# One decoder layer on one core: operand tiles moved to start addresses that differ by multiples of 512 bytes, and parts of two small computations moved off VectorE

## The chip, the cores and the metric

The kernel runs on one core of a Trainium2 chip. The time is that of one execution on the device in microseconds (us); the median of several executions is compared. The engines are named as the profile names them: PE is TensorE's matmuls and PEld its weight loads, DVE is VectorE, ACT is ScalarE, POOL is GpSimd, SP is the queue that issues most DMAs.

## The reference

One decoder layer for 1024 tokens of width 1024, all in float32: two token mixers side by side (a convolution module and an attention with forget gates), a gated sum of both, cross-attention into 256 memory tokens, and a mixture of 16 experts. The two parts that the change rewrites are the layernorm in the convolution module and the logarithm of the forget gates:

```python
def conformer_conv(u_glu, dw_w, dw_b, ln_g, ln_b, pw_w):
    a, gate = jnp.split(u_glu, 2, axis=-1)
    u = a * jax.nn.sigmoid(gate)
    u = lax.conv_general_dilated(u, dw_w[:, None, :], ..., feature_group_count=CONV_DIM) + dw_b
    u = jax.nn.silu(layernorm(u, ln_g, ln_b))
    return u @ pw_w
...
logf = jax.nn.log_sigmoid(f_logit.astype(jnp.float32) + fox_bf[l].astype(jnp.float32))
...
c = jnp.cumsum(logf, axis=1).transpose(0, 2, 1)   # added to the scores of the attention
```

The convolution has 512 channels and 31 taps. The rest of the layer is what the names say: `proj = h @ w_in` gives the inputs of both mixers and their gates, then come `fox_attention`, `cross_attention` and `hierarchical_moe`.

## The kernel before

Activations lie transposed, channels on the 128 partitions and tokens along the row, so that a weight tile of 128x128 is the stationary operand of a matmul and 512 tokens stream past it. Each float32 matrix is split into a rounded part and a rest (`hi` and `lo`, type float32r), and each product is three matmuls (lines 137 to 139: hi by hi, hi by lo, lo by hi). `hh` and `hl` are the two parts of the normed input, 8 tiles each of 4096 bytes per partition; `w_hi` and `w_lo` are the two parts of one weight tile. A column tile of `w_in` is so 2 halves of tokens x 8 x 3 = 48 matmuls of 512 columns. The weight arrives by DMA in `w_raw`; ACT rounds it (line 129), and the rest is subtracted on POOL or DVE (lines 131, 133). `w_hi` and `w_lo` have two buffers each.

Stages in time: the input is read and normed; 19 column tiles of `w_in` (up to about 263 us) for the convolution's input and gate, the convolution's output gate (`gc`), and the first head pair's queries, keys and values; the pointwise product of the convolution (`conv_pw_w`, up to about 312 us); the attention of 8 heads, with the remaining 17 column tiles of `w_in` laid between (up to 666 us); the branch and output products, cross-attention, router and experts.

The convolution runs beside the 19 column tiles. Channels lie in four blocks c = 0 to 3. Blocks 0, 2 and 3 are summed tap by tap on DVE, in PSUM (line 373, `ps_cva<-u,dw_w,ps_cva`). Block 1 is summed in SBUF by a pair: ACT multiplies (line 368, `pj`) and POOL adds (line 369, `oc`). POOL's queue also holds the subtraction of each weight tile (line 131, `w_lo`) and, once, the DMA that stores the running sum of the forget gates (line 417, `c_dram<-ncum`). Each engine works its own queue in order; the order is fixed when the program is built, by a scheduler with priorities, and stands on each engine as shown in the section on the change. DVE also takes every projection's result out of PSUM (line 217, two PSUM buffers `ps_lin`), so a late line 217 holds PE back.

The forget gates (lines 403 to 416) use 8 partitions x 1024 elements: bias, absolute value, exponential, logarithm, correction, and a running sum on DVE. The layernorm (lines 440 to 474) sums the four blocks into `lsum` (442, 443, 448), lets PE sum over partitions (450), subtracts the mean (452), squares on ACT (454, 457), adds the squares up in `lsum` on DVE (458), sums them over partitions with matmuls of one column (462), works out the reciprocal root in small steps (464, 160 to 162, 143 to 145), spreads it over the partitions (468, 470), scales (472), applies silu (473) and splits the result into `yh` and `yl` (474 through 129, 131, 133), which the product with `conv_pw_w` reads.

Where tiles start in SBUF: pools are filled one after the other, each tile behind the last. The small tiles at the head of `hpool` (`g_mem`, `dw_w`, `dw_b`, `ln_g`, `ln_b`, `bf8`: 8, 124, 4, 4, 4 and 1 elements per partition) push all that follows to odd places. Start addresses in the built program, as the remainder by 512: `w_hi` and `w_lo` 256; `hh` and `hl` 416; `ah`, `al` (branch product), the inputs of the cross-attention's query and of half of its output product 480; `yh` 128; `mgh`, `mgl` (output product) 256. In the experts the moving weights `gu` and the stationary `xgT` are both at 480, the moving `dn` is at 256 (for the last expert at 480) and the stationary `uh`, `ul` at 480.

## Time and profile before

| | us |
|---|---|
| three runs | 1240.29, 1238.8, 1247.19 |
| median | 1240.29 |
| the profiled execution | 1246.51 |
| its span (first to last instruction) | 1244.7 |
| mean granted TensorE clock, share of full speed | 0.981 |

The profiled execution holds 1.8 us outside its span and is 6.2 us above the median. Durations below are its own. A matmul's listed time runs from its start to its modelled end and overlaps the next one, so the pace of a stream of matmuls is read from starts. In the windows, busy times of an engine are its instructions' union; a window that PE fills is not proof that PE runs at its best pace. The granted clock is a share of 2.4 GHz: 1.00 is that level, and half of it is the level of 1.2 GHz.

### The profile page before, as it was taken

What the parts mean: (1) busy time and instruction counts of PE and PEld (TensorE: products, weight loads), DVE (VectorE), ACT (ScalarE), POOL (GpSimd) and SP (SyncE); (2) the same over time, 40 slices, a digit from 0 to 9 for tenths busy, and PEclk for the clock granted to TensorE, in tenths of its full rate; (3) what the DMA queues carried; (4) which work ended last, traced back from release to release, by engine and by line L of the source; (5) the groups of instructions that cost most, each with busy time, mean ns of one, the idle gap of its engine ahead of it and who ended that gap; (6) DMA issues with size and microseconds to landing.
All of it is one profiled execution on the core that took longest, in us unless ns stands there. A gap on an engine that the chain in (4) does not pass through costs nothing. (4 is left out here: it accounts for less than half of the span.)

```text
span 1244.7 us, 17029 instructions
## 1 busy us (share of the span) xinstructions
PE 1174.6 (94%) x6125; PEld 908.6 (73%) x6126; DVE 857.4 (69%) x1584; ACT 626.8 (50%) x1057; POOL 397.7 (32%) x270
## 2 busy tenths in 40 slices
PE   7999999989999999999999999999997798999996
PEld 3677877768877777787888787787764576767773
DVE  5499999863978778791234854665887785776665
ACT  6334663531655555472332343552752575776765
POOL 3328994111010010101011575265015023333343
PEclk9999999989999999999999999999998899999999
DMA  5211134126211111111344453234266889999977
GB/s 205 73 38 43 58 102 152 52 84 217 82 58 41 46 55 48 37 47 53 102 135 149 141 162 109 77 111 130 68 201 219 264 241 306 311 311 293 314 181 282
DMA packets 57466, 174.10 MB, mean 140 GB/s; under 512 B 7992, under 2 KB 11080, under 8 KB 57376
## 3 DMA queue, kind: packets, MB, share of 16 engines
q1 hardware_dynamic: 49680, 149.76, 36.2%
q0 software_dynamic: 7696, 23.20, 8.0%
q8 instruction: 50, 0.82, 0.3%
q14 instruction: 40, 0.33, 0.1%
HBM read 136.92 MB, written 36.01 MB: 139 GB/s over the span
## 5 line engine op out<-in xcount | busy, mean ns | idle before, releaser
L131 POOL TENSOR_TENSOR w_lo<-w_raw,w_hi 128x1024 fp32r<-128x1024 f32 x58 | 140.6, 2425 | 471.8 <-ACT w_hi L129 462.0
L137 PE MATMUL ps_lin<-hh,w_hi 128*128 128x512 f32 x560 | 226.5, 404 | 1.0 <-DVE u L351 1.0
L139 PE MATMUL ps_lin<-hh,w_lo 128*128 128x512 f32 x560 | 225.1, 402 | 1.7 <-POOL w_lo L131 1.6
L138 PE MATMUL ps_lin<-hl,w_hi 128*128 128x512 f32 x560 | 226.1, 404 | 0.0
L129 ACT ACTIVATE w_hi<-w_raw 128x1024 fp32r<-128x1024 f32 (+1 forms) x100 | 92.1, 921 | 212.3 <-PE ps_lin L138 158.6
L139 PEld LDWEIGHTS ps_lin<-hh,w_lo 128*128 128x128 f32 x560 | 105.8, 189 | 28.2 <-POOL w_lo L131 3.9
L137 PEld LDWEIGHTS ps_lin<-hh,w_hi 128*128 128x128 f32 x560 | 106.1, 190 | 26.5 <-issue 2.7
L138 PEld LDWEIGHTS ps_lin<-hl,w_hi 128*128 128x128 f32 x560 | 106.0, 189 | 24.8 <-issue 1.8
L373 DVE SCALAR_TENSOR_TENSOR ps_cva<-u,dw_w,ps_cva 128x1024 f32<-128x1024 f32 x90 | 111.7, 1280 | 0.3
L369 POOL TENSOR_TENSOR oc<-oc,pj 128x512 f32<-128x512 f32 x60 | 80.8, 1398 | 14.4 <-ACT pj L368 14.4
L133 DVE SCALAR_TENSOR_TENSOR gu<-e_raw,gu 128x1024 fp32r<-128x1024 f32 x64 | 77.5, 1223 | 4.6 <-ACT gu L129 0.6
L129 ACT ACTIVATE gu<-e_raw 128x1024 fp32r<-128x1024 f32 x64 | 67.5, 1059 | 8.3 <-PE ps_lin L139 6.7
L137 PE MATMUL ps_lin<-gu,xgT 128*128 128x512 f32 x144 | 58.5, 406 | 4.1 <-ACT xgT L129 4.1
L368 ACT ACTIVATE pj<-u,dw_w 128x512 f32<-128x512 f32 x60 | 42.2, 719 | 36.8 <-POOL oc L369 36.7
L133 DVE SCALAR_TENSOR_TENSOR dn<-d_raw,dn 128x1024 fp32r<-128x1024 f32 x32 | 39.0, 1225 | 29.4 <-ACT dn L129 26.8
L557 ACT ACTIVATE sc<-sc,mns 128x128 f32<-128x128 f32 (+3 forms) x64 | 49.4, 773 | 15.7 <-DVE mns L553 15.3
L138 PE MATMUL ps_lin<-gu,xgT 128*128 128x512 f32 x144 | 57.1, 397 | 0.0
L139 PE MATMUL ps_lin<-gu,xgT 128*128 128x512 f32 x144 | 56.9, 395 | 0.0
L133 DVE SCALAR_TENSOR_TENSOR pl<-ps_tra,ph 128x512 fp32r<-128x512 f32 (+1 forms) x80 | 49.1, 636 | 9.8 <-ACT ph L129 8.7
L1294 POOL DMA_INDIRECT xg<-h_dram,ids x29 | 33.2, 1144 | 67.1 <-PE ps_sco L1070 24.3
L129 ACT ACTIVATE ph<-ps_tra 128x512 fp32r<-128x512 f32 (+1 forms) x80 | 41.8, 552 | 23.9 <-PE ps_tra L570 23.1
L570 PE MATMUL ps_tra<-ident,sc 128*128 128x128 f32 x288 | 47.9, 276 | 4.1 <-DVE sc L560 4.1
(475 smaller groups left out, 2860.5 us busy)
## 6 DMA issues: line engine op xcount, KB each, us to landing
e_raw<-in_w_gu SPq DMA_DIRECT2D x64, 512.0 KB
w_raw<-in_w_in SPq DMA_DIRECT2D x36, 512.0 KB
d_raw<-in_w_dn SPq DMA_DIRECT2D x32, 512.0 KB
w_raw<-in_w_out SPq DMA_DIRECT2D x16, 512.0 KB
xT<-in_xT SPq DMA_DIRECT2D x16, 256.0 KB
gc_dram<-gc SPq DMA_DIRECT2D x8, 512.0 KB
gc<-gc_dram SPq DMA_DIRECT2D x8, 512.0 KB
mc_dram<-gc SPq DMA_DIRECT2D x8, 512.0 KB
```

The source lines that it names most:

```text
L129: order["split"] = A.activation(hi, src, AF.Copy, scale=scale)
L131: G.tensor_tensor(lo, src, hi.bitcast(F32), op=OP.subtract)
L133: V.scalar_tensor_tensor(lo, src, scale, hi.bitcast(F32), op0=OP.mult, op1=OP.subtract)
L137: TE.matmul(ps, lh, rh, start=first, stop=False)
L138: TE.matmul(ps, lh, rl, start=False, stop=False)
L139: return TE.matmul(ps, ll, rh, start=False, stop=last)
L368: A.activation(pj, uj, AF.Copy, scale=dw_h[:, c, j:j + 1])
L369: G.tensor_tensor(co[c][:, ns], co[c][:, ns], pj, op=OP.add)
L373: V.scalar_tensor_tensor(sums, u[c][:, j:j + T], dw_h[:, c, j:j + 1], sums, op0=OP.mult, op1=OP.add)
L557: A.activation(sc[:, :nk], sc[:, :nk], AF.Exp, scale=-1.0, bias=mns[:, nch - 1:nch], accum_out=sm)
L570: TE.transpose(pt[:, s_], pr[i][:, blk(j)], ident)
L1294: G.indirect_dma_start(out=XG[e, h][:n], out_offset=None, in_=src, in_offset=bass.IndirectOffsetOnAxis(ap=idx, axis=0))
```

## The change

The small tiles move into one tile `edge` of 56 elements per partition at the right end of SBUF, and `dw_w` is padded to 512 bytes. `mns`, `sm`, `lss` and `xss` get widths or counts that keep later tiles at the same remainder. In the built program nearly all large tiles then start at remainder 256: `hh`, `hl`, `ah`, `al`, `yh`, the cross-attention's inputs, `xgT`, `gu`, `uh`, `ul`, `dn`; `yl` starts at 0, 128, 256 and 384, and `w_hi`, `w_lo`, `mgh`, `mgl` stay at 256. The forget gates' bias, relu and the addition of 1 become ACT's; the addition of the relu becomes the second operand of the running sum. The layernorm's first two sums go to POOL, block 3 is read from PSUM, the squares are no longer added on DVE but each is summed by PE into the same PSUM columns (8 groups of 4 matmuls of one column, before 2 groups), and all eight subtractions that make `yl` go to POOL.

```diff
+    edge = ctx.enter_context(tc.tile_pool(name="edge", bufs=1, side="right")).tile([P, 56], F32, name="edge")
+    g_mem, dw_b, ln_g, ln_b = edge[:, 0:8], edge[:, 8:12], edge[:, 12:16], edge[:, 16:20]
+    bf8, nbf8 = edge[:HEADS, 20:21], edge[:HEADS, 21:22]
...
+    dw_w = hpool.tile([P, 4 * 32], F32, name="dw_w")[:, :4 * TAPS].rearrange("p (c j) -> p c j", c=4)
...
-        V.tensor_scalar(z, z, bf8, None, op0=OP.add)
         e = cv.tile([HEADS, T], F32, name="e", tag="yl", bufs=4)
-        A.activation(e, z, AF.Abs)
+        A.activation(e, z, AF.Abs, bias=bf8)
+        A.activation(z, z, AF.Relu, scale=-1.0, bias=nbf8)
         A.activation(e, e, AF.Exp, scale=-1.0)
         w1 = cv.tile([HEADS, T], F32, name="w1", tag="yl", bufs=4)
-        V.tensor_scalar(w1, e, 1.0, None, op0=OP.add)
+        A.activation(w1, e, AF.Identity, bias=1.0)
         ln = cv.tile([HEADS, T], F32, name="ln", tag="yl", bufs=4)
         A.activation(ln, w1, AF.Ln)
         V.scalar_tensor_tensor(w1, w1, 1.0, e, op0=OP.subtract, op1=OP.subtract)
         V.tensor_tensor(ln, ln, w1, op=OP.subtract)
-        V.tensor_scalar(z, z, -1.0, 0.0, op0=OP.mult, op1=OP.max)
-        V.tensor_tensor(ln, ln, z, op=OP.add)
         ncum = cv.tile([HEADS, T], F32, name="ncum", tag="yl", bufs=4)
-        V.tensor_tensor_scan(ncum, ln, ln, 0.0, OP.add, OP.bypass)
+        V.tensor_tensor_scan(ncum, ln, z, 0.0, OP.add, OP.add)
         G.dma_start(c_dram, ncum)
...
-            V.tensor_tensor(s, co[0], co[2], op=OP.add)
-            V.tensor_tensor(s, s, co[3], op=OP.add)
+            G.tensor_tensor(s, co[0], co[2], op=OP.add)
+            G.tensor_tensor(s, s, co[1], op=OP.add)
...
-                V.tensor_tensor(s[:, ns], s[:, ns], co[1][:, ns], op=OP.add)
+                V.tensor_tensor(s[:, ns], acc[3][:, ns], s[:, ns], op=OP.add)
                 ps = bank("acc")
                 TE.matmul(ps, ones, s[:, ns], start=True, stop=True)
                 for c in range(4):
                     V.scalar_tensor_tensor(co[c][:, ns], ps, -1.0 / 512, co[c][:, ns], op0=OP.mult, op1=OP.add)
+                    sq = cv.tile([P, HALF], F32, name="lsq", tag="pj", bufs=2)
+                    A.activation(sq, co[c][:, ns], AF.Square)
...
-                        V.tensor_tensor(s[:, ns], s[:, ns], sq, op=OP.add)
...
+                        pair = bank("cva", [P, T])
+                        ps2 = pair[:, HALF:]
+                    for t in range(4):
+                        TE.matmul(ps2[:, t:t + 1], sq[:, blk(t)], ones[:, 0:1], start=c + t == 0, stop=c + t == 6)
...
-                    split(yh[c][:, ns], yl[c][:, ns], co[c][:, ns], lo_eng=G if c % 2 else V)
+                    split(yh[c][:, ns], yl[c][:, ns], co[c][:, ns], lo_eng=G)
...
-                    mns = fx.tile([P, 2], F32, name="mns", tag="mns", bufs=4)
+                    mns = fx.tile([P, 16], F32, name="mns", tag="mns", bufs=4)
...
-                    sm = fx.tile([P, 1], F32, name="sm", tag="sm", bufs=4)
+                    sm = fx.tile([P, 16], F32, name="sm", tag="sm", bufs=4)[:, :1]
```

The order of the queues changes in three places that the prediction speaks of. In the changed kernel lines from 76 on are numbered a little higher (131 is there 135, 369 is 373, 417 is 419, 137 to 139 are 141 to 143, 217 is 221).

First, POOL's queue where block 1's taps begin. Before, the DMA of the forget gates' sum stands behind twelve additions:

```order
L131 TENSOR_TENSOR w_lo<-w_raw,w_hi 128x1024 [waits DMAHW2_49,PE_49,Activation_49]
L369 TENSOR_TENSOR oc<-oc,pj 128x512 [waits Activation_49] x4
L131 TENSOR_TENSOR w_lo<-w_raw,w_hi 128x1024 [waits DMAHW3_49,PE_49,Activation_49]
L369 TENSOR_TENSOR oc<-oc,pj 128x512 [waits Activation_49] x8
L417 DMA c_dram<-ncum 8x1024 [waits DMASW0_49,DVE_49]
L131 TENSOR_TENSOR w_lo<-w_raw,w_hi 128x1024 [waits DMAHW4_49,PE_49,Activation_49]
```

Now the same place in the changed kernel:

```order
L135 TENSOR_TENSOR w_lo<-w_raw,w_hi 128x1024 [waits DMAHW2_49,PE_49,Activation_49]
L419 DMA c_dram<-ncum 8x1024 [waits DMASW0_49,DVE_49]
L373 TENSOR_TENSOR oc<-oc,pj 128x512 [waits Activation_49] x2
L135 TENSOR_TENSOR w_lo<-w_raw,w_hi 128x1024 [waits DMAHW3_49,PE_49,Activation_49]
L373 TENSOR_TENSOR oc<-oc,pj 128x512 [waits Activation_49] x10
L135 TENSOR_TENSOR w_lo<-w_raw,w_hi 128x1024 [waits DMAHW4_49,PE_49,Activation_49]
```

The DMA, which waits for DVE, moved ahead of the twelve additions.

Second, DVE's queue at the end of block 3's taps, with the projections' results (`gc`, `qt`) between. Before:

```order
L217 TENSOR_TENSOR gc<-ps_lin,r 128x512
L373 SCALAR_TENSOR_TENSOR ps_cva<-u,dw_w,ps_cva 128x1024
L442 TENSOR_TENSOR lsum<-oc 128x1024
L373 SCALAR_TENSOR_TENSOR ps_cva<-u,dw_w,ps_cva 128x1024 x2
L217 TENSOR_TENSOR gc<-ps_lin,r 128x512
L373 SCALAR_TENSOR_TENSOR ps_cva<-u,dw_w,ps_cva 128x1024 x4
L217 TENSOR_TENSOR gc<-ps_lin,r 128x512
L373 SCALAR_TENSOR_TENSOR ps_cva<-u,dw_w,ps_cva 128x1024
L443 TENSOR_TENSOR lsum<-lsum,oc 128x1024
L448 TENSOR_TENSOR lsum<-lsum,oc 128x512 x2
L217 TENSOR_TENSOR qt<-ps_lin,r 128x512
```

In the changed kernel, from the same half of `gc` (the 14th of 16) on:

```order
L221 TENSOR_TENSOR gc<-ps_lin,r 128x512
L377 SCALAR_TENSOR_TENSOR ps_cva<-u,dw_w,ps_cva 128x1024 x4
L221 TENSOR_TENSOR gc<-ps_lin,r 128x512
L377 SCALAR_TENSOR_TENSOR ps_cva<-u,dw_w,ps_cva 128x1024 x2
L450 TENSOR_TENSOR lsum<-ps_cva,lsum 128x512 x2
L221 TENSOR_TENSOR gc<-ps_lin,r 128x512
L454 SCALAR_TENSOR_TENSOR oc<-ps_acc,oc 128x512 x5
```

Six taps instead of eight stand behind that half, and the layernorm's sum is ready ahead of the 16th half instead of behind it.

Third, PE's queue where the layernorm begins. In the changed kernel the sum over partitions (452) stands 24 matmuls (one half of a column tile) earlier than before, and the squares' matmuls stand singly between projections:

```order
L452 MATMUL ps_acc<-lsum,ones 128x512
L141 MATMUL ps_lin<-hh_110,w_hi 128x512
...
L141 MATMUL ps_lin<-hh_112,w_hi 128x512
L461 MATMUL ps_cva<-ones,lsq 128x1 x4
L142 MATMUL ps_lin<-hl_120,w_hi 128x512
L143 MATMUL ps_lin<-hh_112,w_lo 128x512
L141 MATMUL ps_lin<-hh_113,w_hi 128x512
L461 MATMUL ps_cva<-ones,lsq 128x1 x4
```

Before, 117 projection matmuls stand between the first of these sums and the first matmul of `conv_pw_w`; now 141 do, and eight groups `128x1 x4` instead of two.

## Rows read from the trace of the kernel before

**Rows 1.** Page: busy time, share of span, count; and the costliest DVE group.
```profile
PE 1174.6 (94%) x6125; PEld 908.6 (73%) x6126; DVE 857.4 (69%) x1584; ACT 626.8 (50%) x1057; POOL 397.7 (32%) x270
...
L373 DVE SCALAR_TENSOR_TENSOR ps_cva<-u,dw_w,ps_cva 128x1024 f32<-128x1024 f32 x90 | 111.7, 1280 | 0.3
```

**Rows 2.** Windows: stretch, length, PE, PEld, DVE, ACT, POOL busy, clock, DMA share, GB/s.
```profile
125.00:187.00 62.00, 61.92 (x265) 49.50 (x264) 58.28 (x56) 38.35 (x57) 61.57 (x46) 1.00 0.27 77
...
250.00:262.00 12.00, 7.87 (x27) 5.18 (x25) 10.98 (x22) 8.16 (x15) 2.93 (x2) 0.86 0.09 22
262.00:312.00 50.00, 49.15 (x212) 39.97 (x213) 17.16 (x27) 8.73 (x13) 5.25 (x3) 0.97 0.55 189
312.00:480.00 168.00, 161.16 (x913) 129.93 (x913) 136.40 (x351) 95.53 (x206) 15.29 (x7) 0.99 0.18 51
...
1060.00:1215.00 155.00, 153.48 (x1164) 112.45 (x1162) 103.08 (x125) 107.89 (x163) 55.21 (x38) 1.00 0.94 281
```

**Rows 3.** Groups of PE, 716 to 750, 670 to 710, 140 to 187 us: count, busy, mean ns.
```profile
L137 PE MATMUL ps_lin<-mgh,w_hi 128*128 128x512 f32 x50 | 19.4, 389 | 0.0
...
L137 PE MATMUL ps_lin<-ah,w_hi 128*128 128x512 f32 x57 | 22.5, 396 | 0.0
...
L137 PE MATMUL ps_lin<-hh,w_hi 128*128 128x512 f32 x67 | 26.6, 396 | 0.0
```

**Rows 4.** Timeline of PE, the first and last L137 of 716 to 750 us.
```profile
716.10 0.39 PE L137 MATMUL ps_lin<-mgh,w_hi 128*128 128x512 f32 x1
...
749.42 0.39 PE L137 MATMUL ps_lin<-mgh,w_hi 128*128 128x512 f32 x1
```

**Rows 5.** Groups of PE in the experts: 1060 to 1215, then the last expert.
```profile
L138 PE MATMUL ps_lin<-dn,uh 128*128 128x512 f32 x44 | 17.4, 395 | 0.0
...
L138 PE MATMUL ps_lin<-dn,uh 128*128 128x512 f32 x4 | 1.6, 391 | 0.0
```

**Rows 6.** Timeline: start, length; POOL's queue from 119 us on, PE's wait at 192.
```profile
119.65 2.42 POOL L131 TENSOR_TENSOR w_lo<-w_raw,w_hi 128x1024 fp32r<-128x1024 f32 x1
...
142.91 10.11 POOL L369 TENSOR_TENSOR oc<-oc,pj 128x512 f32<-128x512 f32 x8
...
192.63 0.50 PE L139 MATMUL ps_lin<-hh,w_lo 128*128 128x512 f32 x1 [0.87 <-POOL w_lo L131]
```

**Rows 7.** Timeline of DVE: forget gates, then the end of the taps.
```profile
90.29 2.10 DVE L408 TENSOR_SCALAR w<-e 8x1024 f32<-8x1024 f32 x1
...
103.07 3.11 DVE L412 TENSOR_TENSOR ln<-ln,w 8x1024 f32<-8x1024 f32 x1
...
109.04 2.77 DVE L416 TENSOR_TENSOR_SCAN ncum<-ln 8x1024 f32<-8x1024 f32 x1
...
203.71 0.69 DVE L217 TENSOR_TENSOR gc<-ps_lin,r 128x512 f32<-128x512 f32 x1 [1.30 <-PE ps_lin L139]
...
205.59 2.56 DVE L442 TENSOR_TENSOR lsum<-oc 128x1024 f32<-128x1024 f32 x1
...
219.38 1.23 DVE L443 TENSOR_TENSOR lsum<-lsum,oc 128x1024 f32<-128x1024 f32 x1 [1.15 <-ACT oc L382]
```

**Rows 8.** Timeline of PE, from the layernorm's first sum to the pointwise product.
```profile
221.55 1.10 PE L450 MATMUL ps_acc<-lsum,ones 128*128 128x512 f32 x2 [0.30 <-DVE lsum L448]
...
236.22 1.05 PE L462 MATMUL ps_cva<-ones,lsum 128*128 128x1 f32 x8 [0.60 <-DVE lsum L458]
...
252.96 1.11 PE L317 MATMUL ps_tra<-ident,qt 128*128 128x128 f32 x4 [2.42 <-DVE qt L217]
...
262.85 0.84 PE L317 MATMUL ps_tra<-ident,qt 128*128 128x128 f32 x4 [2.57 <-DVE vs L133]
263.34 0.78 PE L137 MATMUL ps_lin<-yh,w_hi 128*128 128x512 f32 x1
```

**Rows 9.** Timeline of ACT at the forget gates: the exponential, the logarithm's table.
```profile
86.53 1.06 ACT L406 ACTIVATE e<-e 8x1024 f32<-8x1024 f32 x1
...
89.39 1.28 ACT L410 ACT_TABLE_LOAD   x1
```

More of the change, by code (lines that the diff above doesn't have):

```diff
@@ L111, in small @@
         return t
-    g_mem = small("g_mem", a["norm_mem_g"], [P, KD])
+    G.dma_start(g_mem, a["norm_mem_g"])
     g_mix = consts.tile([P, KD], F32, name="g_mix")
@@ L117, in layer_kernel @@
     g_moe = small("g_moe", a["norm_moe_g"], [P, KD], consts)
-    dw_w = small("dw_w", a["conv_dw_w"], [P, 4, TAPS])
-    dw_b = small("dw_b", a["conv_dw_b"], [P, 4])
-    ln_g = small("ln_g", a["conv_ln_g"], [P, 4])
-    ln_b = small("ln_b", a["conv_ln_b"], [P, 4])
-    bf8 = small("bf8", a["fox_bf"], [HEADS, 1])
+    dw_w = hpool.tile([P, 4 * 32], F32, name="dw_w")[:, :4 * TAPS].rearrange("p (c j) -> p c j", c=4)
+    G.dma_start(dw_w, a["conv_dw_w"])
+    for t_, src_ in ((dw_b, "conv_dw_b"), (ln_g, "conv_ln_g"), (ln_b, "conv_ln_b"), (bf8, "fox_bf")):
+        G.dma_start(t_, a[src_])
+    V.tensor_scalar(nbf8, bf8, -1.0, None, op0=OP.mult)
     dw_h = dw_w
@@ L452, in layer_kernel @@
                     V.scalar_tensor_tensor(co[c][:, ns], ps, -1.0 / 512, co[c][:, ns], op0=OP.mult, op1=OP.add)
+                    sq = cv.tile([P, HALF], F32, name="lsq", tag="pj", bufs=2)
+                    A.activation(sq, co[c][:, ns], AF.Square)
                     if c == 0:
-                        A.activation(s[:, ns], co[0][:, ns], AF.Square)
-                    else:
-                        sq = cv.tile([P, HALF], F32, name="lsq", tag="pj", bufs=2)
-                        A.activation(sq, co[c][:, ns], AF.Square)
-                        V.tensor_tensor(s[:, ns], s[:, ns], sq, op=OP.add)
-                pair = bank("cva", [P, T])
-                ps = pair[:, HALF:]
-                for t in range(4):
-                    TE.matmul(ps[:, t:t + 1], s[:, blk(4 * n + t)], ones[:, 0:1], start=True, stop=True)
-                ss = cv.tile([P, 4], F32, name="lss", tag="lss", bufs=2)
+                        pair = bank("cva", [P, T])
+                        ps2 = pair[:, HALF:]
+                    for t in range(4):
+                        TE.matmul(ps2[:, t:t + 1], sq[:, blk(t)], ones[:, 0:1], start=c + t == 0, stop=c + t == 6)
+                ps = ps2
+                ss = cv.tile([P, 4], F32, name="lss", tag="lss", bufs=7)
                 V.tensor_copy(ss, ps[:, :4])
@@ L699, in w_out @@
             TE.matmul(ps[:, t:t + 1], acc[:, blk(t)], ones[:, 0:1], start=True, stop=True)
-        ss = xa.tile([P, 4], F32, name="xss", tag="xss", bufs=2)
+        ss = xa.tile([P, 4], F32, name="xss", tag="xss", bufs=3)
         V.tensor_copy(ss, ps[:, :4])
```

## The prediction

> **What bounds the kernel now.** I read the page's busy times first: PE is busy 94% of the span, DVE 69%, ACT 50%, POOL 32% [rows 1]. So I look for two things only: how fast PE streams when nothing holds it, and where something does hold it. The windows come next: in 125 to 187 us PE has no gap worth naming, 62 us hold 265 matmuls at clock 1.00, which is 0.234 us each; the stretch 250 to 262 us is the weak one, PE busy 7.87 of 12 us and the clock at 0.86, and the following 50 us have 0.97 [rows 2]. The groups by operand then show that matmuls of one shape differ: 389 ns each with `mgh` streaming, 396 with `ah` or `hh` [rows 3]. The listed time overlaps the next matmul, so only the difference counts, 7 ns. The pace itself comes from starts: first and last listed `mgh` matmul lie 33.32 us apart with 49 x 3 = 147 matmuls between, 0.2267 us each [rows 4], against the 0.234 of `hh` [rows 2]. At a granted clock of 1.00 in both, that is 3% of a full-rate stream.
>
> What tells the fast from the slow is the subject of the change. `mgh` and `w_hi` both start at remainder 256; `hh` lies at 416 and `ah` at 480 against weights at 256. The sharpest pair is in the experts: `dn` against `uh`, same line, shape and neighbours, takes 395 ns while `dn` is at 256 and `uh` at 480, and 391 in the last expert, where both are at 480 [rows 5]. So it is the difference of the two addresses that matters, not either address alone. That one stretch is short (4 matmuls), and 256 against 512 as the unit isn't told apart by it; either way nearly all pairs of the changed kernel are on the fast side.
>
> The timelines show the holds before the pointwise product: POOL's queue of additions and `w_lo` subtractions, busy 61.57 of 62 us in 125 to 187 us [rows 2], ends in a PE wait for `w_lo` at 192 us [rows 6]; DVE then ends block 3's taps and the sums [rows 7]; PE meets the layernorm's sums and four visible waits [rows 8].
>
> **Step 1: up to PE's wait for `w_lo` at 192 us.** PE's some 700 matmuls on `hh` between 20 and 187 us get 7 ns faster each, about 5 us. PE can't keep all of that, because POOL is the bound at the end of this stretch: PE goes on at 192.63, when a `w_lo` is ready [rows 6], and POOL had no pause since 125 [rows 2]. So I follow POOL. Its DMA of the forget gates' sum now stands ahead of the twelve additions and waits for DVE's scan, which ended at 109.04 + 2.77 = 111.8 [rows 7]. The chain before the scan changes so: ACT's exponential ended at 87.6 [rows 9]; it now comes 0.7 us sooner by the bias that left DVE and 1.06 later by the relu, then the addition of 1 takes 1.06 on ACT, the table 1.28 and the logarithm about 1.06 [rows 9]: 91.3. Behind it DVE does one subtraction (3.11 as before, though beside POOL), a result of 0.69, a tap of 1.28 and the scan, 2.77 [rows 1, 7], 7.9 us: 99.1, of which I take 98.8, since the subtraction then stands beside an idle POOL. POOL then has the DMA (0.5), twelve additions at 10.11 / 8 = 1.26 and one subtraction of 2.42 [rows 6], 18.1 us, and begins at 116.9 the `w_lo` that it began at 119.65 before [rows 6]. From there on the queue is as before, so 2.75 us are gained, and 3 with some short waits for `pj`: PE goes on at 189.5. Bounds: 192.6 if the wait eats it all, 186.7 if POOL is no limit and PE keeps its own 5 us and the 0.87.
>
> The ACT operations that the chain gained are priced in it. ACT rounds one weight tile behind them instead of between them, 3 us later; the cover is that a tile lasts PE 48 x 0.2267 = 10.9 us and two are held. If that cover were gone, PE would lose those 3 us.
>
> **Step 2: to the layernorm's first sum on PE.** Before, 120 matmuls lie between PE's wait and the sum at 221.55 (192.63 + 120 x 0.234 = 220.7, and waits). Now 96 do, since the sum stands 24 matmuls earlier: 189.5 + 96 x 0.2267 = 211.3. DVE must be ready by then: its 14th half of `gc`, at 203.71 before, comes at 199.8 (3.1 us from step 1, 0.8 from what comes faster behind it), and behind it stand six taps at 1.28 [rows 1], one result of 0.69 and the half sum, some 0.7 [rows 7], so 208.9. What left that queue are two taps, the 2.56 and 1.23 us of the first sums, and the 1.15 us wait for ACT's copy of block 3 [rows 7]. The two sums that POOL takes in their place, some 2.4 us each (it reads and writes as much as for a `w_lo` of 2.42 [rows 6]), have as cover that POOL's taps end there; if POOL were late with them, 2 to 3 us would be lost here.
>
> **Step 3: from that sum to the pointwise product.** Before 263.34 - 221.55 = 41.8 us [rows 8]: 117 matmuls at 0.234 make 27.3, the waits 0.60, 2.42 and 2.57 make 5.6 [rows 8], the rest, 8.9, is the sums' own matmuls, transposes, and the lower clock of 0.86 over 12 us, 1.7 us [rows 2]. After: 141 matmuls at 0.2267 are 32.0; the rest without the slow clock 7.2; six more groups of squares at 1.05 (the row of the group: four matmuls, listed as eight) [rows 8] are 6.3; and 1.0 for small waits. That is 46.5. The product starts at 211.3 + 46.5 = 257.8, 5.5 us earlier.
>
> That the waits go is a choice. They stand behind DVE's results `qt` and the split of `vs` [rows 8], where DVE is busy 10.98 of 12 us; it loses the six additions of squares and four subtractions of `yl`, ten instructions of about 0.7 us, 7 us in all. POOL, with 2.93 of 12 busy [rows 2], has room for all eight subtractions at half of 2.42 [rows 6]. If the two long waits stay, 5 us of the gain are lost, and the clock's 1.7 with them. What is late next is the reciprocal root's chain, as long as before, from its last square on.
>
> **Step 4: behind 258 us.** Here PE is busy 161.16 of 168 us [rows 2], so most of a pace gain arrives. The 17 column tiles laid into the attention hold 17 x 48 = 816 matmuls: 816 x 7 ns [rows 3] = 5.7, of which I take 5.0, since attention's waits eat some. The pointwise product has 192 matmuls, of which those on `yh` become aligned to `w` and those on `yl` in half the tiles; 4 ns on average, 0.8. Branch product, 192 x 7 ns [rows 3], 1.2. Cross-attention's query and half of its output, 270 matmuls, 1.7. The experts' `dn` at half of 184 x 6 ns, 0.5, because the DMA share there is 0.94 [rows 2]; `gu` is aligned to `xgT` before and after, nothing. The transposed value products 0.2. The clock of 0.97 over the 50 us behind the product's start [rows 2] is worth 1.5, and I take 1.7 with its neighbours, as the hole in PE's work that came before it is closed. Sum 11.1.
>
> **Sum.** 5.5 + 11.1 = 16.6 us. The profiled execution took 1246.5, so 1229.9, a ratio of 0.9867; that execution lies 6.2 above the median, and the ratio on the median of 1240.3 gives 1224. Of it 9.4 us are the pace behind 258 us, 3.2 at most the clock, and the rest what the start of the product gains.
>
> **Rivals.** *The remainders do nothing.* The pace may come from what else the operands share: `hh` is read while POOL and DVE are full [rows 2], `mgh` at a quiet place. For it: two of my three pairs differ in surroundings also. Against: the `ah` stretch, right before the `mgh` one, is as slow as `hh` [rows 3], and `dn` changes in the same loop [rows 5]. Then step 2 gives 189.5 + 96 x 0.234 = 212.0, step 3 141 x 0.234 + 14.1 = 47.1, the product starts at 259.1, 4.2 gained, and 1.7 of clock behind it: 5.9, or 1234. The Trainium skill, "TensorE: Matmul & The Clock Gate", section "Step-by-step: what each phase is for", states that TensorE reads the SBUF through two independent read ports, one for the streaming operand and one for the weights; by that rule the address of one should not matter to the other, and the time would be this rival's. The `dn` rows speak against it.
>
> *A wait takes the place of the ones removed.* Each of the eight squares now is a link ACT to PE in PE's own order, with two buffers `lsq` for eight tiles shared with `pj`, and every projection matmul stands behind it. If each group waits a microsecond, as the `lsum` group did 0.60 [rows 8], 8 us go, and the product starts 2.5 us later than before. Of the 16.6 us 8.6 are left: 1232. For it: ACT feeds eight squares, the centred blocks come from DVE one by one. Against: 24 more projection matmuls lie between as cover.
>
> *The other side: POOL's queue is held by the DMA.* POOL stands in order behind the scan. If the chain of ACT and DVE links ends late, at t, every `w_lo` behind it is late, and PE, with two buffers, stops: `w_lo` comes at 189.5 + (t - 98.8). The gain of steps 1 to 4 is gone when the product starts 11.1 later than before, at 274.4, which is `w_lo` at 206.1 and t = 115.4, later than the old 111.8. At t = 120 it is 1245 on the median, at t = 130 1255. For it: POOL has nothing to give up in 125 to 187 us [rows 2], and the DMA moved past twelve additions. Against: the chain has lost four DVE operations and gained two ACT ones.
>
> **How the numbers follow.** Forecast 0.70, no alignment effect 0.12, waits at the squares 0.13, the held queue 0.05. The forecast's own range is 1216 to 1232 (step 1's bounds are worth 3 each way, the waits of step 3 another 5, the shares of step 4 about 3). The range of 8 in 10 takes in the first two rivals with their own spread above, and below the case that all bounds fall well together (186.7 in step 1, no small waits in step 3, full shares in step 4), with 2 us at each end since three runs of one kernel differ by 8: 1213 to 1238. One per cent, 12.4 us, is about what a measurement of this kernel can tell from no change. Of the forecast's chance 0.62 lies below 1227.9, of the others 0.06: faster 0.68; the same 0.28; slower 0.04, most of it the held queue with t beyond 128.
>
> **What would show it.** Right: groups on `hh` at 389 to 390 ns a matmul and 0.227 from start to start; `dn` at 391 in all experts; `gu` unchanged; PE's last wait for `w_lo` at about 189.5; the first sum on PE at 211; the product's start near 258; clock at 0.97 or above in 250 to 312. Wrong: `hh` still at 396 (first rival); PE waits over half a microsecond at each group of squares (second); POOL idle for over 5 us before the DMA and later `w_lo` (third). The forecast fails as a whole if the stretches behind 312 us don't shrink by about 9 us together.

## The result and the profile after

The changed kernel takes 1235.3 us, median of nine executions (1230.95 to 1240.98), the kernel before 1246.16 beside it (nine, 1238.8 to 1252.21). The ratio is 0.9924, 95% interval 0.9901 to 0.9946: 0.0076 of the 1240.3 us that the forecast started from are 9.4 us less, where 16.6 were forecast (ratio 0.9867). On that base the changed kernel takes 1230.9 us: inside the forecast's 1213 to 1238, above the 1227.9 below which it put most of its chance. In two later series it came out at 0.9919 [0.9886, 0.9951] and 0.9945 [0.9927, 0.9964].

The page's rows that answer to [rows 1]; the tap is line 377 now:

```profile
PE 1158.4 (94%) x6173; PEld 908.2 (74%) x6174; DVE 840.8 (68%) x1569; ACT 629.5 (51%) x1059; POOL 403.2 (33%) x276
...
L377 DVE SCALAR_TENSOR_TENSOR ps_cva<-u,dw_w,ps_cva 128x1024 f32<-128x1024 f32 x90 | 111.6, 1279 | 0.5
```

PE has 16 us less to do at the same share. The windows, with the stretches of [rows 2] and one more (columns as there):

```profile
125.00:187.00 62.00, 60.69 (x267) 49.61 (x265) 58.41 (x56) 39.60 (x59) 61.57 (x45) 1.00 0.26 85
250.00:262.00 12.00, 10.00 (x47) 7.76 (x46) 7.21 (x12) 3.60 (x8) 0.00 (x0) 1.00 0.08 23
262.00:312.00 50.00, 49.97 (x228) 40.93 (x227) 18.73 (x41) 10.72 (x20) 4.78 (x2) 1.00 0.62 211
312.00:480.00 168.00, 160.74 (x930) 130.24 (x929) 139.29 (x349) 97.34 (x207) 14.43 (x6) 1.00 0.16 48
1060.00:1215.00 155.00, 151.39 (x1143) 111.00 (x1143) 100.58 (x140) 106.13 (x166) 55.59 (x37) 1.00 0.92 279
235.00:240.00 5.00, 3.04 (x5) 1.82 (x6) 4.94 (x7) 3.36 (x6) 4.53 (x4) 0.70 0.02 3
```

In 262 to 312 us, 228 matmuls go where 212 went, at clock 1.00. Neither dip of the clock stands where [rows 2] has it (0.86 and 0.97 in 250 to 312 us), but a new one of 0.70 stands in 235 to 240 us, where PE is busy 3.04 of 5 us. POOL is as full in 125 to 187 us as it was.

The groups of PE that answer to [rows 3] (140 to 187 us, 660 to 704, 705 to 740), and the experts' line 142 to [rows 5] (1060 to 1199 us):

```profile
L141 PE MATMUL ps_lin<-hh,w_hi 128*128 128x512 f32 x67 | 26.1, 389 | 0.0
...
L141 PE MATMUL ps_lin<-ah,w_hi 128*128 128x512 f32 x64 | 24.9, 389 | 0.0
...
L141 PE MATMUL ps_lin<-mgh,w_hi 128*128 128x512 f32 x52 | 20.2, 389 | 0.0
...
L142 PE MATMUL ps_lin<-dn,uh 128*128 128x512 f32 x40 | 15.6, 391 | 0.0
```

`hh` and `ah` are at the pace that only `mgh` had, `dn` at that of the last expert. The timeline of PE answers to [rows 6] and [rows 8]: the wait for `w_lo`, the layernorm's first sum, the products with `diag` (line 470, of which [rows 8] shows none, as they had no wait), the transposes, the pointwise product:

```profile
187.46 0.50 PE L143 MATMUL ps_lin<-hh,w_lo 128*128 128x512 f32 x1 [1.20 <-POOL w_lo L135]
...
209.60 1.02 PE L452 MATMUL ps_acc<-lsum,ones 128*128 128x512 f32 x2
212.08 1.04 PE L461 MATMUL ps_cva<-ones,lsq 128*128 128x1 f32 x8
...
236.96 2.08 PE L470 MATMUL ps_cva<-diag,ones 128*128 128x512 f32 x2 [2.57 <-DVE diag L468]
254.81 0.66 PE L321 MATMUL ps_tra<-ident,qt 128*128 128x128 f32 x4 [1.22 <-DVE qt L221]
260.36 0.66 PE L321 MATMUL ps_tra<-ident,qt 128*128 128x128 f32 x4 [0.79 <-DVE qt L221]
...
260.77 0.48 PE L141 MATMUL ps_lin<-yh,w_hi 128*128 128x512 f32 x1
```

The first sum comes 12 us sooner than before (221.55), the pointwise product 2.6 (263.34). Between the two a new wait of 2.57 us stands, for `diag`. What DVE and POOL do in front of it:

```profile
230.32 2.20 DVE L148 SCALAR_TENSOR_TENSOR lnt<-lnt,lnv 128x4 f32<-128x4 f32 x1
...
235.03 1.88 DVE L468 TENSOR_SCALAR diag<-ident,lnr 128x128 f32<-128x128 f32 x4
236.94 3.35 DVE L295 SCALAR_TENSOR_TENSOR qs<-qt,qs 64x512 fp32r<-64x512 f32 x2
...
230.11 2.40 POOL L135 TENSOR_TENSOR w_lo<-w_raw,w_hi 128x1024 fp32r<-128x1024 f32 x1 [17.64 <-ACT w_hi L133]
...
235.47 5.97 POOL L135 TENSOR_TENSOR yl<-oc,yh 128x512 fp32r<-128x512 f32 x4 [2.97 <-ACT yh L133]
```

An operation on 128x4 elements, 0.16 us elsewhere in the same chain, takes 2.20: it begins just behind POOL's subtraction of a weight tile and ends with it. The last of the four operations of `diag` is held too: beside the first `yl` it takes 1.29 of their 1.88 us. The kernel before had the same, and the prediction passed it by; DVE's and POOL's timelines of before, where a 128x4 operation on a single tile also took 1.61 us beside a `w_lo` that ran from 229.54 to 231.94:

```profile
230.36 1.61 DVE L160 TENSOR_SCALAR lnv<-lss 128x4 f32<-128x4 f32 x1
...
248.01 1.27 DVE L143 TENSOR_TENSOR lnt<-lnr 128x4 f32<-128x4 f32 x1
...
247.96 1.29 POOL L131 TENSOR_TENSOR yl<-oc,yh 128x512 fp32r<-128x512 f32 x1 [16.02 <-ACT yh L129]
```

### The profile page after: what moved, and what is told of

Its sections match the earlier page's. It is cut to its first block, busy times and chain, and to the rows that moved or that the text cites. A ratio compares the mean times of both kernels' runs of the same rounds, so it can differ in the third digit from the quotient of the medians.

```text
span 1229.5 us, 17120 instructions
## 1 busy us (share of the span) xinstructions
PE 1158.4 (94%) x6173; PEld 908.2 (74%) x6174; DVE 840.8 (68%) x1569; ACT 629.5 (51%) x1059; POOL 403.2 (33%) x276
## 5 line engine op out<-in xcount | busy, mean ns | idle before, releaser
L143 PE MATMUL ps_lin<-hh,w_lo 128*128 128x512 f32 x560 | 222.5, 397 | 2.3 <-POOL w_lo L135 2.2
L141 PE MATMUL ps_lin<-hh,w_hi 128*128 128x512 f32 x560 | 222.9, 398 | 0.7 <-DVE u L355 0.6
L142 PE MATMUL ps_lin<-hl,w_hi 128*128 128x512 f32 x560 | 221.7, 396 | 0.0
L137 DVE SCALAR_TENSOR_TENSOR gu<-e_raw,gu 128x1024 fp32r<-128x1024 f32 x64 | 77.5, 1222 | 4.7 <-ACT gu L133 1.0
L373 POOL TENSOR_TENSOR oc<-oc,pj 128x512 f32<-128x512 f32 x60 | 76.0, 1323 | 8.8 <-ACT pj L372 8.7
L137 DVE SCALAR_TENSOR_TENSOR dn<-d_raw,dn 128x1024 fp32r<-128x1024 f32 x32 | 39.1, 1227 | 27.8 <-ACT dn L133 27.7
L557 ACT ACTIVATE sc<-sc,mns 128x128 f32<-128x128 f32 (+3 forms) x64 | 49.4, 773 | 15.6 <-DVE mns L553 15.2
L137 DVE SCALAR_TENSOR_TENSOR pl<-ps_tra,ph 128x512 fp32r<-128x512 f32 (+1 forms) x80 | 49.1, 636 | 9.3 <-ACT ph L133 8.2
```

The lines of the kernel that those rows point to most:

```text
L137: V.scalar_tensor_tensor(lo, src, scale, hi.bitcast(F32), op0=OP.mult, op1=OP.subtract)
L141: TE.matmul(ps, lh, rh, start=first, stop=False)
L142: TE.matmul(ps, lh, rl, start=False, stop=False)
L143: return TE.matmul(ps, ll, rh, start=False, stop=last)
L373: G.tensor_tensor(co[c][:, ns], co[c][:, ns], pj, op=OP.add)
L557: A.activation(sc[:, :nk], sc[:, :nk], AF.Exp, scale=-1.0, bias=mns[:, nch - 1:nch], accum_out=sm)
```

## The experiments

Each kernel's profile gives the start of the pointwise product (first matmul on `yh`), the last `hh` matmul, the first of the experts (`gu`) and the span, in us. Ratios are to the kernel before, timed beside each.

| kernel | ratio [95%] | product | last hh | first gu | span |
|---|---|---|---|---|---|
| before | 1 | 263.3 | 661.3 | 972.0 | 1244.7 |
| changed | 0.9924 [0.9901, 0.9946] | 260.8 | 651.6 | 957.2 | 1229.5 |
| e3, same | 0.9919 [0.9886, 0.9951] | 261.3 | 652.0 | 962.9 | 1230.6 |
| e10, same | 0.9945 [0.9927, 0.9964] | 260.4 | 652.6 | 961.6 | 1233.8 |
| e1 addresses | 0.9937 [0.9905, 0.9969] | 260.4 | 652.3 | 961.4 | 1233.8 |
| e2 engine moves | 0.9998 [0.9972, 1.0023] | 263.5 | 659.7 | 972.5 | 1243.6 |
| e11 addresses, gates | 0.9935 [0.9913, 0.9957] | 259.9 | 652.0 | 961.3 | 1239.8 |
| e12 addresses, layernorm | 0.9996 [0.9971, 1.0022] | 266.0 | 656.7 | 967.5 | 1235.3 |
| e7 hh 256 off, ah 128 | 0.9952 [0.9925, 0.9978] | 260.8 | 653.0 | 965.6 | 1234.5 |
| e8 64 off | 0.9957 [0.9936, 0.9978] | 262.7 | 655.1 | 962.3 | 1229.5 |
| e4 root in PSUM | 0.9916 [0.9881, 0.995] | 260.3 | 651.1 | 960.9 | 1235.4 |
| e5 squares on DVE | 0.9912 [0.9877, 0.9946] | 259.1 | 651.4 | 962.8 | 1238.8 |
| e6 yl shared | 0.994 [0.9912, 0.9968] | 261.4 | 652.2 | 962.1 | 1236.2 |
| e9 late half | 0.9957 [0.994, 0.9973] | 262.1 | 653.0 | 963.6 | 1236.0 |
| b1 = e4 + e5 | 0.9908 [0.9889, 0.9927] | 257.5 | 648.6 | 957.7 | 1228.4 |
| b5, same as b1 | 0.9902 [0.9865, 0.9939] | 257.1 | 648.2 | 957.4 | 1229.1 |
| b3 = b1 + e9 | 0.9948 [0.9927, 0.9969] | 259.1 | 651.5 | 960.6 | 1231.5 |
| b4 = e11 + root in PSUM | 0.9948 [0.9926, 0.9969] | 260.1 | 653.7 | 962.8 | 1238.7 |
| b6 = b1 + ident in PSUM | 0.99 [0.9874, 0.9926] | 254.6 | 646.7 | 956.0 | 1227.3 |

The experts' stretch (first `gu` to the end) lies between 267 and 279 us whatever was edited ahead of it: the changed kernel itself has 272.3, 267.7 and 272.2. So the span of one profile says less than the columns before it.

**Addresses or engine moves (e1, e2, e3, e10).** e1 takes over only the placement, e2 all but the placement:

```diff
 e1, on the kernel before
+    edge = ...tile([P, 56], F32, name="edge")
+    dw_w = hpool.tile([P, 4 * 32], F32, name="dw_w")...
 (and the sizes of mns, sm, lss, xss)
 e2, on the changed kernel: those edits undone
```

Expected of e1: 

> Only the placement of the change (edge tile, padded dw_w, mns, sm, lss, xss); every engine's order is that of before. My theory (the pace follows the difference of the two operand addresses): matmuls on hh, ah, h, o, dn at 0.227 us from start to start instead of 0.234, PE's wait for w_lo near 192 stays since POOL bounds it, so about 2 us are gained up to the pointwise product and 9 to 10 behind it: 11 us, ratio 0.991. Rival (remainders do nothing, the engine moves made the gain): hh stays at 0.234, ratio 1.000.

Expected of e2: 

> Only the engine moves of the change, with the old addresses (remainders as before); every engine's order is that of the changed kernel. My theory: hh at 0.234, PE's last wait for w_lo some 3 to 5 us earlier, the eight groups of squares give 6 us of it back, nothing gained behind 312 us: 2 to 5 us in all, ratio 0.996 to 0.998. Rival (remainders do nothing): the whole gain, ratio 0.992. With e1 and the changed kernel this makes a table of two by two; if the parts add up, the two gains sum to that of the changed kernel.

Expected of e3: 

> The changed kernel once more, for a second profile and more timed executions on the chip of e1, e2 and e4. Theory: the profiled 1231 us was one of the quicker executions and the typical one is 1235, ratio 0.992; where an execution is slower its mean granted clock is lower (0.980 against 0.988). Rival: the profile is typical and the ratio comes out at 0.988.

Expected of e10: 

> The changed kernel a third time, beside the three above on one chip, as their base and for a third profile. Theory: ratio 0.992, and the profiles of one kernel differ mostly between 860 us and the end (waits for experts' data and the router's chain, with the clock that goes with them), not ahead of it: start of the product within 0.5 us of 260.8 and 261.3, last matmul of line 143 on h within 3 us. Rival: the difference of 6 us between its profile's gain and its median's gain lies in the stretch that the change touches.

The addresses alone give the ratio 0.9937, the moves alone 0.9998. The product starts 3.0 us sooner by the addresses and no sooner by the moves (263.46). From there to the last `hh` matmul before took 397.9 us, e1 392.0, e2 396.2, the changed kernel 390.8. So the remainders do something, and the engine moves as a whole nothing that shows; for the moves 0.996 to 0.998 was expected, a miss. So was e1's wait for `w_lo`, which was to stay near 192 us:

```profile
189.85 0.50 PE L142 MATMUL ps_lin<-hh,w_lo 128*128 128x512 f32 x1 [1.16 <-POOL w_lo L134]
```

In e2 PE waits for no `w_lo` there at all. Of e3 and e10 the profiled executions ran 1 and 4 us longer than the first. Up to 753 us the three agree within about 1 us; at 773 us e3 is 3.4 and e10 1.9 us later, so the differences begin there, ahead of the 860 us that were expected.

**Which multiple (e7, e8).** The orders are those of the changed kernel; a few tiles' sizes move the addresses.

```diff
 e7: hh, yh at 0 by 512; ah, h, o, uh at 384; w_hi, dn at 256
-    ...tile([P, 56], F32, name="edge")
+    ...tile([P, 24], F32, name="edge")
-    dw_w = hpool.tile([P, 4 * 32], ...
+    dw_w = hpool.tile([P, 192], ...
-    lss bufs=7, mns [P, 16]
+    lss bufs=3, mns [P, 2]
 e8: hh, yh, ah, h, o, uh at 320: edge [P, 40], dw_w [P, 144]
```

Expected of e7: 

> The changed kernel's orders with other addresses: hh, hl and yh at remainder 0 by 512, so 256 away from w_hi and w_lo; ah, h, o (384 against 256) and dn against uh 128 away; mgh stays. Theory (what counts is the difference by 256, as the rows of yl in the changed kernel suggest): matmuls on hh and yh keep 0.227 us from start to start, those on ah, h, o and dn go to 0.233; the time rises by 2 to 4 us against the changed kernel. Rival (by 512, as the change's words say): hh goes to 0.234 and the time to that of e2, 1245.

Expected of e8: 

> The changed kernel's orders, with hh, hl, yh, ah, h and o 64 bytes away from w_hi and w_lo by 512, and dn 64 away from uh. Theory (any difference that is no multiple of 256 costs some 6 to 7 ns a matmul): all of them at 0.231 to 0.234 us, and the time that of the engine moves alone, about 1245, ratio 1.00. Rival (only some differences cost, those of 96 to 160 and 224 to 416 that the kernel before has): 0.227 us stays and so does the time.

Groups of PE in e7, 140 to 187 us and 659 to 707:

```profile
L141 PE MATMUL ps_lin<-hh,w_hi 128*128 128x512 f32 x67 | 26.1, 389 | 0.0
...
L141 PE MATMUL ps_lin<-ah,w_hi 128*128 128x512 f32 x64 | 25.3, 395 | 0.0
```

256 bytes apart is as good as 512; 128 apart costs 6 ns. The changed kernel shows it by itself: its four `yl` tiles start at 0, 128, 256 and 384 against `w_hi` at 256, and its matmuls on them take 395 and 389 ns by turns. In e8, 64 apart, three lines of `ah`:

```profile
L142 PE MATMUL ps_lin<-al,w_hi 128*128 128x512 f32 x64 | 25.2, 394 | 0.0
L141 PE MATMUL ps_lin<-ah,w_hi 128*128 128x512 f32 x64 | 25.1, 392 | 0.0
L143 PE MATMUL ps_lin<-ah,w_lo 128*128 128x512 f32 x64 | 24.8, 388 | 0.0
```

They differ by line, 2.3 ns above 389 on average, about a third of the full loss; `dn`, 64 from `uh`, is at 395 (1060 to 1199 us), as slow as in the kernel before. The time, 0.9957, lies between the changed kernel and the moves alone. Both expectations for e8 missed: 64 costs, on `ah` less than 128.

**Which of the moves (e11, e12, b4).** e11 has the new addresses and the forget gates' lines of the change, with the layernorm's block as before; e12 the reverse.

```diff
 e11, on the changed kernel: the layernorm's block of the kernel before
 e12, on e1: the layernorm's block of the changed kernel
 b4, on e11: the root's small tiles in PSUM (as e4 below)
```

Expected of e11: 

> The new addresses and the forget gates' part of the change alone; the layernorm stands as in the kernel before. Theory (the gates' part frees POOL and DVE early, the layernorm's part gives that back): PE's last wait for w_lo ends at 187 to 188 us as in the changed kernel (189.8 with the addresses alone), the layernorm's wait for qt stays at about 2.5 us twice, the product starts at 258 to 260, 1 to 3 us before that of the addresses alone (260.35). Rival (the gates' part brings nothing, since DVE's row of taps sets the layernorm's first sum): 260.3.

Expected of e12: 

> The new addresses and the layernorm's part of the change alone; the forget gates stand as in the kernel before. Theory: the eight groups of squares and the wait for diag cost what the shorter waits for qt give, so the product starts 1 to 3 us after that of the addresses alone, at 261.5 to 263.5. Rival: the layernorm's part is what helps, the product starts before 260.

Expected of b4: 

> e11 with the root's small tiles in PSUM. Theory (in the kernel before too, one 128x4 operation of the root took 1.27 us beside POOL): 1 to 2 us less than e11 at the product's start, 257 to 259; not better than b1. Rival: without POOL's longer block of subtractions the root is not held, and the start is that of e11.

In e11 the wait for `w_lo` ends at 188.5, near what was expected, but PE then stands before the first sum, so the product starts only 0.5 us sooner than in e1, nearer to the rival:

```profile
188.54 0.50 PE L143 MATMUL ps_lin<-hh,w_lo 128*128 128x512 f32 x1 [1.19 <-POOL w_lo L135]
...
214.93 1.89 PE L452 MATMUL ps_acc<-lsum,ones 128*128 128x512 f32 x2 [1.84 <-DVE lsum L450]
```

In e12 the product starts 5.6 us later than in e1, more than expected: the first sum comes at 216.3 (e1: 218.46), then eight groups of 0.95 us stand where two stood, and `diag` is waited for:

```profile
233.47 2.39 DVE L148 SCALAR_TENSOR_TENSOR lnr<-lnt,lnr 128x4 f32<-128x4 f32 x1
...
238.90 1.90 PE L471 MATMUL ps_cva<-diag,ones 128*128 128x512 f32 x2 [2.56 <-DVE diag L469]
```

So the layernorm's part loses by itself, and beside it the gates' part gives about the same again: from e12 to the changed kernel the first sum comes 6.7 us sooner (216.30 to 209.60), 3.3 of it at the wait for `w_lo` (190.73 to 187.46), the rest by standing about 15 matmuls further ahead in PE's order. That it gives little in e11 because DVE's sums bound PE there fits the wait of 1.84 us, but no run separates it. In b4 the root was not what bounded the old layernorm; the rival held.

**What holds DVE (e4, e6, e9).** e4 puts two of the root's three small tiles into PSUM, so that none of its operations reads two operands from SBUF:

```diff
+    v, t = ps2[:, 64:68], ps2[:, 128:132]
-            newton(r, v, t)
+            V.tensor_tensor(t, v, r, op=OP.mult)
+            V.scalar_tensor_tensor(t, t, -0.5, r, op0=OP.mult, op1=OP.mult)
+            V.scalar_tensor_tensor(r, t, 1.5, r, op0=OP.add, op1=OP.mult)
 e6: split(..., lo_eng=G if c % 2 else V)
 e9: silu and split of the second half stand behind the block with priority
```

Expected of e4: 

> The changed kernel, with two of the three small tiles of the layernorm's reciprocal root in PSUM and its products in another order, so that no operation of that chain reads two operands from SBUF. Theory (DVE's two-operand operations are held while POOL subtracts, as the 128x4 operation that took 2.20 us beside a w_lo): none of the chain's operations takes over 0.5 us, PE's wait of 2.57 us before the second product with diag shrinks below 1 us, the clock of 0.70 in 235 to 240 us goes to about 0.9 or more, and the time falls by 2 to 4 us against the changed kernel, ratio to before about 0.989 to 0.990. Rival (the delay is DVE's order, or something that POOL does to all of DVE): the long operation stays and the time is that of the changed kernel.

Expected of e6: 

> The changed kernel, with the subtractions that make yl shared between POOL and DVE as before. Theory (POOL's subtractions hold DVE's operations with two operands in SBUF): POOL is busy about 5 us less in 230 to 250 us, DVE does four operations of 0.7 us more, its two qs subtractions (3.35 us beside POOL) are shorter, and the two cancel: the start of the product within 1.5 us of 260.8, the time within 2 us of the changed kernel. Rival (moving all eight to POOL was the part of the change that helps): the product starts 3 us later.

Expected of e9: 

> The changed kernel with only that last edit: the second half's silu and split behind the keys. Theory (the diag wait comes first in PE's order, so a later wait that goes brings little): the two qt waits (1.2 and 0.8 us) shrink, the diag wait of 2.6 us stays, the product starts within 2 us of 260.8. Rival (ACT's order is what delays diag too): the diag wait shrinks by over 1 us.

e4's DVE, POOL and PE (line 176 is the root's second step):

```profile
232.79 0.16 DVE L176 SCALAR_TENSOR_TENSOR ps_cva<-ps_cva,lnr 128x4 f32<-128x4 f32 x1
...
231.81 2.40 POOL L135 TENSOR_TENSOR w_lo<-w_raw,w_hi 128x1024 fp32r<-128x1024 f32 x1 [18.51 <-ACT w_hi L133]
...
252.30 1.12 PE L330 MATMUL ps_tra<-ident,qt 128*128 128x128 f32 x4 [3.34 <-DVE qt L230]
```

The same step beside the same subtraction takes 0.16 us, and both waits for `diag` are gone. The product starts only 0.5 us sooner all the same, so the 2 to 4 us that were expected of the time are not seen, and its ratio can't be told from the changed kernel's: a wait of 3.34 us for `qt` came up, behind ACT's silu and rounding, and the clock's dip went with it (1.00 in 235 to 240 us, 0.72 in 250 to 255). e6 moved nothing (261.4), as expected: its root is held for the same 2.20 us beside the weight tile, and it waits 2.75 us for `diag`. So giving POOL all eight subtractions of `yl` isn't what made that wait. e9 kept its wait for `diag`, as expected, but its waits for `qt` didn't shrink (1.68 and 0.79 us), and its product starts 1.3 us later.

**A better version (e5, b1, b3, b5, b6).** e5 adds up the squares on DVE again; b1 is e4 and e5 together, b5 the same kernel again, b3 b1 with e9's edit, b6 b1 with a copy of `ident` in PSUM:

```diff
 e5, on the changed kernel
+                        V.tensor_tensor(s[:, ns], s[:, ns], sq, op=OP.add)
-  eight groups of four matmuls on sq
+  two groups of four matmuls on s
 b6, on b1
+                        A.activation(ps2[:, 256:384], ident, AF.Copy)
-                    V.tensor_scalar(dg[:, t], ident, inv[:, t:t + 1], ...
+                    V.tensor_scalar(dg[:, t], ps2[:, 256:384], inv[:, t:t + 1], ...
```

Expected of e5: 

> The changed kernel, with the layernorm's squares added up on DVE again: two groups of one-column matmuls on PE instead of eight, six additions of 0.7 us more on DVE. Theory (the eight groups cost PE 0.95 us each, the six more give back what the shorter waits gain): the stretch from the first sum to the pointwise product, 51.2 us in the changed kernel, shortens by up to 5.7 us if the waits stay as they are, so the product starts at 255 to 257 and the time falls by 3 to 5 us. Rival (DVE and ACT set the start of the product, PE's groups only fill time in which it would wait): the groups go, the waits for diag and qt grow by as much, and the start stays within 1 us of 260.8.

Expected of b1: 

> The two edits of e4 and e5 together: the root's small tiles in PSUM and the squares added on DVE. Theory (each alone ended in the wait that the other removes: e5 in 1.6 and 4.1 us for diag, e4 in 3.3 us for qt): the diag waits fall below 2 us together, the product starts at 256 to 258, 3 to 4 us before that of the changed kernel (260.8), and the time falls by as much, ratio to before 0.988 to 0.990. Rival (ACT's queue of silu and rounding, which stands ahead of the keys, sets the start): the wait for qt grows to 5 us or more and the product starts at 259 or later.

Expected of b3: 

> As b1, and the silu and the split of the second half of tokens stand behind the keys' operations on ACT and POOL, as they were in the kernel before. Theory (with the diag waits gone, ACT's block of silu and rounding between 233 and 246 us keeps the keys late, and so qt's buffers): the wait for qt falls below 1.5 us, the product starts at 254 to 256, the time falls by 5 to 7 us against the changed kernel, ratio to before 0.986 to 0.988. Rival (PE's own work fills the stretch by now): the same start as b1.

Expected of b5: 

> b1 once more. Theory: the product starts at 257.5 within 0.5 us, and the ratio to before is 0.989 to 0.991, below that of the changed kernel (0.992 to 0.9945 in its three series). Rival: b1's quick series was chance, and this one comes out at 0.993 or more.

Expected of b6: 

> b1, with a copy of ident in PSUM from which diag is made, so that this operation too reads SBUF through nothing but its column of scalars. In b1 four of these operations took 2.62 and 3.25 us where POOL was subtracting, against 0.88 elsewhere. Theory (POOL holds them, as it holds operations with two operands in SBUF, and lets go those with an operand in PSUM): both groups take about 0.9 us, PE's waits for diag (0.90 and 2.81 us in b1) lose about 2 us, and the product starts at 255 to 257 (257.5 and 257.1 in b1). Rival (they are slow because their scalars or their place in the queue come late): the groups stay above 2 us and the start where it is.

In e5 six groups left PE, 5.7 us, and the start gained 1.7, between what theory and rival had; the waits for `diag` grew to 1.64 and 4.06. Its DVE beside POOL's four subtractions:

```profile
233.42 1.08 DVE L148 SCALAR_TENSOR_TENSOR lnt<-lnt,lnv 128x4 f32<-128x4 f32 x1
234.54 1.21 DVE L149 SCALAR_TENSOR_TENSOR lnr<-lnt,lnr 128x4 f32<-128x4 f32 x1
235.78 1.19 DVE L147 TENSOR_TENSOR lnt<-lnr 128x4 f32<-128x4 f32 x1
237.00 1.18 DVE L148 SCALAR_TENSOR_TENSOR lnt<-lnt,lnv 128x4 f32<-128x4 f32 x1
...
233.19 4.98 POOL L135 TENSOR_TENSOR yl<-oc,yh 128x512 fp32r<-128x512 f32 x4 [5.69 <-ACT yh L133]
```

One step of the root gets through per subtraction, 4.98 / 4 = 1.25 us each. b1 frees the root, and the product starts at 257.5, as expected; but the operation that makes `diag` is still held, and the waits for it, 0.90 and 2.81 us, are together above the 2 us expected. b6 frees that too. DVE's line 480 in b1, then line 481 in b6:

```profile
235.73 3.25 DVE L480 TENSOR_SCALAR diag<-ident,lnr 128x128 f32<-128x128 f32 x4
```

```profile
233.85 1.13 DVE L481 TENSOR_SCALAR diag<-ps_cva,lnr 128x128 f32<-128x128 f32 x4
```

With both freed, no wait for `diag` is left, and the product starts at 254.6, 6.2 us before that of the changed kernel; a wait of 3.61 us for `qt` remains. b1's two series and b6 took 1229.6, 1231.5 and 1231.0 us, 0.990 to 0.991 of before, where the changed kernel had 0.992 to 0.9945: better than the changed kernel by about 4 us, though the intervals of most of these series overlap. That b6 beats b1 is seen in its trace up to 650 us, not in the times. b3 was a miss: its edit costs b1 1.6 us at the start.

The Trainium skill, "SBUF — State Buffer", section "🔬 SBUF: two separate sides", says that DVE and GpSimd share one pair of ports by an exclusive lock, held for a whole instruction, and that a DVE operation needs it when it has two inputs in SBUF or runs in a two-port mode. The traces agree: 2.20 us beside one subtraction of 2.40, 0.16 with an operand in PSUM. That `diag`, with one tile in SBUF, runs in such a mode is not shown; that it is held, and freed by PSUM, is.

## Why the prediction was wrong

**What held.** The pace follows the difference of the addresses: `hh` and `ah` went to 389 ns, `dn` to 391, as forecast, and the first rival falls (e1). The Trainium skill, "TensorE: Matmul & The Clock Gate", section "Step-by-step: what each phase is for", states that TensorE reads the streaming operand and the weights through two independent read ports. That doesn't account for these runs: 389 or 396 ns goes by both operands' addresses together. Step 1 put the scan's end at 98.8 us, it came at 96.9, and PE went on at 187.5 (189.5 forecast). With the old addresses (e2) the scan ended at 98.2, so 1.2 us of that difference are the faster pace ahead of the gates, which step 1 left out of this chain. Step 2 put the first sum at 211.3; it came at 209.6. The held queue, third rival, did not happen: POOL did stand idle for over 5 us before the DMA, but the `w_lo` behind the twelve additions began 4.5 us sooner than the 119.65 of [rows 6].

```profile
97.22 0.54 POOL L419 DMA_DIRECT2D c_dram<-ncum  x1 [7.69 <-DVE ncum L418]
...
115.17 2.38 POOL L135 TENSOR_TENSOR w_lo<-w_raw,w_hi 128x1024 fp32r<-128x1024 f32 x1
```

**What failed: step 3.** "1.0 for small waits" and "the rest without the slow clock" made 46.5 us from the first sum to the product. It took 260.77 - 209.60 = 51.2. The waits are 0.29 and 2.57 for `diag`, 1.22 and 0.79 for `qt`: 4.9 us, 3.9 more than forecast. The dip that step 3 took out only changed its place: 0.70 over 5 us is 1.5 us lost again. Smaller terms gave 0.7 back, such as the groups of squares at 0.95 us where 1.05 was put. The wait for `diag` came about like this. The prediction called the root's chain "as long as before, from its last square on" and put no wait on it. Before, from the last square's matmul (237.0) to the last of `diag` (253.7), it took 16.7 us, and PE came to the product with `diag` later still, behind 14.9 us of other work and the wait of 2.42 for `qt`. In the changed kernel PE has about 9 us of other work left there. The chain takes 11.8 (225.1 to 236.9), of which 2.0 are the held step and 1.0 the held `diag`; in e4, where the root isn't held, it takes 9.0, and PE doesn't wait. The prediction asked whether POOL had room for eight subtractions, and it had; it didn't ask what DVE could do beside POOL, though step 1 had taken 0.3 us off a subtraction because POOL was idle. Nor was the second rival right as put: no group of squares shows a wait in the trace; the wait came behind them. With that, the moves as a whole were worth nothing at the product's start (e2) where the first rival's working, which had them alone, put 4.2 us: the layernorm's part costs 5.6 (e12), the gates' part gives that back. (That working's 14.1 for the terms besides the matmuls should be 14.5 by step 3's own terms.) That the product's start missed by 3.0 us and not by the 4.7 of step 3 is luck: steps 1 and 2 were 1.7 too late.

**Step 4, 11.1 forecast.** The pointwise product's stretch, first `yh` to last `yl`, went from 45.5 to 43.4 us, 2.0 where 0.8 + 1.7 was put. From there to the last `hh` it went from 352.5 to 347.4: 5.1, against 5.0. Branch product, first to last `ah`: 44.6 to 43.3, 1.3 against 1.2. The 1.7 for the cross-attention didn't show: first to last `h` took 113.1 us before and 111.3, 113.9 and 112.3 in the three profiles of the changed kernel, so the profiles of one kernel differ by more than the gain. Nor can the experts' 0.5 be seen.

**From the profile to the median.** Up to 753 us the three profiles of the changed kernel are 10.3, 10.1 and 9.9 us ahead of the one of before, where 14.2 were forecast: 3.0 are missing at the product's start and about 1 behind it. At the end of their spans they are 15.2, 14.1 and 10.9 ahead, but the ratio of the timed runs makes 9.4. The profile of before took 1246.5, up to 5 us above its medians in the series (1241.3 to 1246.2), those of the changed kernel 1231.4, 1232.4 and 1235.6 with medians of 1235.3, 1236.3 and 1235.65. Which executions were profiled can so account for what the spans show beyond the timed gain; I scaled by the ratio where I should have put that spread into the time. Whether the 2.4 us forecast behind 753 us came at all can't be settled from these runs, since profiles of one kernel differ there by up to 5.7 us.

## What to carry to other kernels

Where a kernel is bound by streaming 512-column matmuls, look up the start addresses of the moving and the stationary tile in the built program: a difference that is a multiple of 256 bytes ran 3% faster here than differences of 128, 160 or 224, and a padded tile is all it takes. Before a small chain on DVE is put on PE's path, list what POOL does at that time, the subtractions that were always there too: operations whose tiles all lie in SBUF were held here until POOL's instruction ended, 2.2 us for one of 0.16; an operand in PSUM let them through. And when several waits stand in a row on one engine's path, take away two or three in one trial before judging any: e4 and e5 gave 0.5 and 1.7 us at the product's start, together 3.3, and with b6's edit 6.2.

## What was not expected of the hardware

The loss is no matter of aligned or not: 64 bytes off cost 0 to 5 ns by line of `ah` (388 to 394 against 389), 128 bytes 6 ns, 256 nothing. And a DVE operation with one SBUF tile and a column of scalars (`diag`) took 3.25 us for four beside POOL, 0.88 elsewhere; with its tile in PSUM 1.13. The hold goes both ways. In the kernel before, an addition on POOL that takes 1.26 us elsewhere ([rows 6]) took 3.28, ending 1.1 us behind DVE's scan on two SBUF operands (109.04 to 111.81, [rows 7]):

```profile
109.62 3.28 POOL L369 TENSOR_TENSOR oc<-oc,pj 128x512 f32<-128x512 f32 x1
```

Four of block 1's additions beside the forget gates' operations on DVE were 4.9 us longer together than such additions elsewhere; in the changed kernel none of the twelve behind the DMA is.
